# Feed-forward stages that start on tokens not yet normed, in a two-layer decoder trunk

## The chip, the cores and the metric

The kernel runs on one core of one Trainium2 chip. The metric is the device time of one execution in microseconds (us), as the median of several runs. The engines of the core are named as in the profile: PE (matrix products and transposes; PEld is its loading of weights), DVE (vector engine), ACT (scalar engine), POOL (GpSimd), SP (the engine whose queue issues the loads from memory).

## What is computed

The input is 256 tokens of 1024 values in float32. Two layers follow each other; each has a feed-forward stage, a token mixer, and a second feed-forward stage. Cut to what matters here:

```python
def rmsnorm(x, g):
    y = x * lax.rsqrt(jnp.mean(x * x, axis=-1, keepdims=True) + 1e-6)
    return y * g

def swiglu(h, w_gate, w_up, w_down):          # 1024 -> 2816 -> 1024
    return (jax.nn.silu(h @ w_gate) * (h @ w_up)) @ w_down

for layer in range(2):
    f = swiglu(rmsnorm(x, g[0]), w_gate[layer, 0], w_up[layer, 0], w_down[layer, 0])
    x = x + 0.5 * rmsnorm(f, g[1])
    x = x + rmsnorm(mixer(rmsnorm(x, g[2])), g[3])
    f = swiglu(rmsnorm(x, g[4]), w_gate[layer, 1], w_up[layer, 1], w_down[layer, 1])
    x = x + 0.5 * rmsnorm(f, g[5])
```

So there are four feed-forward stages. Below they are the first (layer 0, ahead of the mixer), the second (layer 0, behind it), the third (layer 1, which follows the second with no mixer between) and the fourth. The factor 1/rms is one number for each token, and it can be applied before the product with `w_gate` and `w_up` or to the rows of its result.

## The kernel before

**Tiles.** The tokens lie in two halves (t = 0, 1) of 128 tokens by 1024 values. For a product the tokens must stand transposed: 8 blocks of 128x128. Every product in full precision is made of three products of a coarse part (`hi`) and a remainder (`lo`): `mm3` (L144 to L147) issues them. ACT makes each `hi` as a rounded copy and DVE makes each `lo` as the difference: for weights in `split_raw` (L96, L97; 128x1024 at a time, a *unit*), for tokens in `split` (L157, L158).

**Weights.** A piece of weights (1 MB) is loaded into one of 5 raw buffers (`raw`), and its two units go to buffers `hi` and `lo`, of which there are 9 each (`NW`). A unit's buffer is free again when the last product that reads it is done.

**A feed-forward stage** (`ffn`, L250) goes over 11 chunks of 256 columns of `w_gate` and `w_up`. `GU(t, c)` (L269) is the product of one half with one chunk, 24 PE matmuls of 512 columns; `both` (L253) is the same for both halves. `gated` (L279) takes the result: Silu on ACT, a multiply on DVE (L285, or L287 where it applies 1/rms itself), giving `h`. `T` (L290) transposes `h` on PE and splits it, and `Dn` (L298) is the 12 matmuls of its product with `w_down` (rows `f<-hi_dn,hs`). Pairs of chunks (2, 3), (5, 6) and (8, 9) are done by seven products instead of eight, `M(i, a)` with i = 0 to 6 (L338), 12 matmuls each: their factors are sums of token blocks, made once for each stage by `sums` (L315: four additions L319 and four splits into `S1` to `S4`, the last in the buffer `tg`), and sums of weight blocks, made on DVE for each pair (L358, L359, L374, L382: 128x2048 each) and then split in their turn (rows `lo_t`). Results are combined on DVE too (L364, L372, L379).

The second to fourth stage begin with `GU(0,0), GU(0,1), T(0,0), Dn(0,0), GU(1,0), T(0,1), GU(1,1), T(1,0), Dn(0,1)`; then comes `M(0, 2)`, which calls `sums`. The first stage begins with `both(0), both(1)`, two `T`, and `M(0, 2)`.

**Norms.** When the last product of a stage or mixer for one half is done, `tail` (L844) calls `post_norm` (L222), which ends in the new tokens `x` (L237). Then, ahead of a feed-forward stage, `ffn_norm` (L185) runs: ACT sums the squares (L192), `rstd_of` (L179) makes 1/rms with a small DVE operation (L181) and a power on POOL (L182), ACT multiplies the tokens by it (L197), PE transposes the result (8 transposes, L153), DVE multiplies by the norm's gain `g` (L201, four 128x512 in all for both halves), and `split` gives `hi` and `lo` in `xh0/xl0` or `xh1/xl1`. The tiles from L201 are kept (`whole`) for `sums`. Ahead of a mixer, `pre_norm` (L206) transposes the tokens as they are, and the mixer applies 1/rms to its products. The first stage does both: `both(0)` runs on the tokens of `pre_norm`, in the buffers `S1`, `S2`, `S3` and `tg`, with 1/rms applied in `gated` (L287); behind it `ffn_norm` (given the ready 1/rms) makes the normed ones, and all else uses these.

**The order.** The list of `GU`, `M`, `T` and `Dn` comes from the planner in `ffn` (`price`, `settle`), and it is the same whatever happens in the norms. When the kernel is built, a scheduler gives every engine a fixed list of instructions: it plays the program through with durations of its own, and an engine that is free takes the earliest-written instruction whose inputs and output buffer are reckoned ready. So an instruction can be moved ahead of earlier-written ones that aren't ready. On the chip each engine follows its list in order.

**Elsewhere.** The conformer part of the even mixer scales its transposed channels by a number for each token with a product of the kind that the change adds: a diagonal matrix from DVE (L590), a PE product with a matrix of ones (L591), and a DVE multiply that reads the result with a broadcast (L592). The ones are a part of the constants, loaded by `small_loads` (L808) in the first stage.

Of the kernel before, what the change touches and what calls it, by code (L numbers as in the profile page):

```python
# [10 lines left out]
F32 = mybir.dt.float32  # L11
F32R = mybir.dt.float32r
BF16 = mybir.dt.bfloat16
AF = mybir.ActivationFunctionType
ALU = mybir.AluOpType
AX = mybir.AxisListType

P = 128
D = 1024
KD = D // P  # L20
# [9 lines left out]
PRE_SCALE = 1.0 / 32.0  # L30
# [9 lines left out]
C_ID, C_ONES, C_MEAN, C_CAUSW, C_ROPE, C_MNEG, C_MSTRICT = 0, 128, 256, 384, 512, 768, 1024  # L40
C_KEEP, C_END = 768, 1280
# [7 lines left out]
def trunk(ctx, tc, x, norm_g, w_gate, w_up, w_down, ab_in, ab_out, conv_w, conv_b, conv_g, conv_bb,  # L49
          cd_in, cd_out, sgu_g, sgu_b, sgu_w, sgu_bs, consts, out):  # L50
    nc = tc.nc
    cp = ctx.enter_context(tc.tile_pool(name="cp", bufs=1))
    wp = ctx.enter_context(tc.tile_pool(name="wp", bufs=1))
    sp = ctx.enter_context(tc.tile_pool(name="sp", bufs=1))
# [8 lines left out]
    def ps_tr(name):  # L63
        return pp.tile([P, 512], F32, tag="tr", name=name, bufs=2)

    xs = [cp.tile([P, D], F32, name=f"x{t}") for t in range(2)]
    cst = cp.tile([P, C_KEEP], F32, name="cst")
    ident = cst[:, C_ID:C_ID + P]
    ones = cst[:, C_ONES:C_ONES + P]
# [2 lines left out]

    mhalf = cp.tile([P, 1], F32, name="mhalf")
    nc.gpsimd.memset(mhalf, -0.5)

    early = cp.tile([P, 1], F32, name="early")
    nc.scalar.activation(early, mhalf, AF.Silu)
# [71 lines left out]
    def transposes(src, name, n=4):  # L149

        ps = ps_tr(name)
        for i in range(n):
            nc.tensor.transpose(ps[:, i * P:(i + 1) * P], src[:, i * P:(i + 1) * P], ident)  # L153
        return ps

    def split(ps, hi, lo):
        nc.scalar.activation(hi, ps, AF.Copy)  # L157
        nc.vector.tensor_tensor(lo, ps, f32v(hi), op=ALU.subtract)  # L158

    def xT_tiles(t, name):  # L160
        hi = sp.tile([P, KD, P], F32R, tag=f"xh{t}", name=f"xh{t}_{name}")
        lo = sp.tile([P, KD, P], F32R, tag=f"xl{t}", name=f"xl{t}_{name}")
        return hi, lo


    def in_turn(dst, src):

        tc.keep_in_program_order(nc.sync.dma_start(dst, src))
# [10 lines left out]
    def rstd_of(s, eps, name):  # L179
        v = sp.tile([P, 2], F32, tag="rv", name=f"v_{name}", bufs=4)  # L180
        nc.vector.tensor_scalar(v[:, 0:1], s[:, 0:1], s[:, 1:2], eps, op0=ALU.add, op1=ALU.add)  # L181
        nc.gpsimd.tensor_tensor(v[:, 1:2], v[:, 0:1], mhalf, op=ALU.pow)  # L182
        return v[:, 1:2]

    def ffn_norm(t, gi, name, r=None):  # L185

        hi, lo = xT_tiles(t, name)
        if r is None:
            s = sp.tile([P, 2], F32, tag="rs", name=f"s2_{name}{t}", bufs=4)
            for j in range(2):  # L190
                junk = sp.tile([P, 512], F32, tag="y", name=f"j2{j}_{name}{t}", bufs=2)
                nc.scalar.activation(junk, xs[t][:, j * 512:(j + 1) * 512], AF.Square, scale=PRE_SCALE, accum_out=s[:, j:j + 1])  # L192
            r = rstd_of(s, 1e-6, f"p{name}{t}")
        whole = []
        for j in range(2):
            y = sp.tile([P, 512], F32, tag="y", name=f"y{j}_{name}{t}", bufs=2)
            nc.scalar.activation(y, xs[t][:, j * 512:(j + 1) * 512], AF.Copy, scale=r)  # L197
            ps = transposes(y, f"xT{j}_{name}{t}")
            a = sp.tile([P, 512], F32, tag="tok", name=f"a{j}_{name}{t}", bufs=4)
            gk = gT[:, gi * KD + 4 * j:gi * KD + 4 * j + 4, None].to_broadcast([P, 4, P])  # L200
            nc.vector.tensor_tensor(a.rearrange("p (a b) -> p a b", b=P), ps.rearrange("p (a b) -> p a b", b=P), gk, op=ALU.mult)  # L201
            split(a, hi[:, 4 * j:4 * j + 4].rearrange("p a b -> p (a b)"), lo[:, 4 * j:4 * j + 4].rearrange("p a b -> p (a b)"))
            whole.append(a)
        return hi, lo, None, whole

    def pre_norm(t, gi, name):  # L206

        s = sp.tile([P, 2], F32, tag="rs", name=f"s2_{name}{t}", bufs=4)
        hi, lo = xT_tiles(t, name) if gi else [sp.tile([P, KD, P], F32R, tag=tag, name=f"{tag}_{name}{t}", bufs=1) for tag in (("S1", "S2"), ("S3", "tg"))[t]]
        for j in range(2):  # L210
            ps = transposes(xs[t][:, j * 512:(j + 1) * 512], f"xT{j}_{name}{t}")
            y = sp.tile([P, 512], F32, tag="y", name=f"y{j}_{name}{t}", bufs=2)
            gk = gT[:, gi * KD + 4 * j:gi * KD + 4 * j + 4, None].to_broadcast([P, 4, P])
            nc.vector.tensor_tensor(y.rearrange("p (a b) -> p a b", b=P), ps.rearrange("p (a b) -> p a b", b=P), gk, op=ALU.mult)
            split(y, hi[:, 4 * j:4 * j + 4].rearrange("p a b -> p (a b)"), lo[:, 4 * j:4 * j + 4].rearrange("p a b -> p (a b)"))
        for j in range(2):
            c = slice(j * 512, (j + 1) * 512)
            junk = sp.tile([P, 512], F32, tag="y", name=f"j2{j}_{name}{t}", bufs=2)
            nc.scalar.activation(junk, xs[t][:, c], AF.Square, scale=PRE_SCALE, accum_out=s[:, j:j + 1])
        return hi, lo, rstd_of(s, 1e-6, f"p{name}{t}"), None  # L220

    def post_norm(t, acc, g, half, name, last=False):  # L222

# [26 lines left out]
    def ffn(l, j, pre, tail, hooks=()):  # L250
        gu_u, dn_u, hT, acc = {}, {}, {}, {}

        def both(_, c):  # L253

            gu_u[c] = prep_gu(l, j, c)
            if 1 not in pre:
                pre[1] = pre_norm(1, 0, "l0f0")
            ps = [ps_mm(f"gu{l}{j}_{t}_{c}") for t in range(2)]
            for u in range(0, KD, 2):
                for t in range(2):  # L260
                    for k in (u, u + 1):
                        mm3(ps[t], pre[t][0][:, k, :], pre[t][1][:, k, :], *gu_u[c][k], k == 0, k == KD - 1)
            for t in range(2):
                gated(t, c, ps[t])
            if (l, j, c) == (0, 0, 0):
                for t in range(2):
                    pre[t] = ffn_norm(t, 0, "l0n", pre[t][2])

        def GU(t, c):  # L269
            if c not in gu_u:  # L270
                gu_u[c] = prep_gu(l, j, c)
            hi, lo = pre[t][0:2]
            ps = ps_mm(f"gu{l}{j}_{t}_{c}")
            for k in range(KD):
                wh, wl = gu_u[c][k]
                mm3(ps, hi[:, k, :], lo[:, k, :], wh, wl, k == 0, k == KD - 1)
            gated(t, c, ps)

        def gated(t, c, ps):  # L279
            r = pre[t][2]  # L280
            sg = sp.tile([P, FC], F32, tag="p", name=f"sg{l}{j}_{t}_{c}", bufs=2)
            nc.scalar.activation(sg, ps[:, 0:FC], AF.Silu, scale=1.0 if r is None else r)  # L282
            h = sp.tile([P, FC], F32, tag="pts", name=f"h{l}{j}_{t}_{c}", bufs=2)
            if r is None:
                nc.vector.tensor_tensor(h, ps[:, FC:2 * FC], sg, op=ALU.mult)  # L285
            else:
                nc.vector.scalar_tensor_tensor(h, ps[:, FC:2 * FC], r, sg, op0=ALU.mult, op1=ALU.mult)  # L287
            hT[t, c] = h
# [515 lines left out]
    def small_loads():  # L804

        for n in range(1, 6):
            in_turn(*g_rows(n))
        in_turn(cst[:, P:C_KEEP], consts[:, P:C_KEEP])  # L808
        masks = sp.tile([P, 512], F32, tag="tok", name="masks", bufs=4)
        in_turn(masks[:, 0:C_END - C_KEEP], consts[:, C_KEEP:C_END])  # L810
        nc.gpsimd.tensor_copy(mneg, masks[:, 0:2 * P])
        nc.gpsimd.tensor_copy(mstrict, masks[:, 2 * P:4 * P])
        small["cw"] = sp.tile([P, 512], F32, tag="tok", name="cw_sb", bufs=4)
        in_turn(small["cw"][0:TAPS, :], conv_w[0])
        small["cv"] = sp.tile([12, P], F32, tag="dg", name="cv_sb", bufs=2)
        for i, vv in enumerate((conv_b, conv_g, conv_bb)):
            in_turn(small["cv"][4 * i:4 * i + 4], vv[0].rearrange("(a b) -> a b", b=P))
        small["sw"] = sp.tile([P, 4, P], F32, tag="tok", name="sw_sb", bufs=4)
        in_turn(small["sw"], sgu_w[0].rearrange("g t s -> t g s"))
        small["sb"] = sp.tile([4, P], F32, tag="dg", name="sbt_sb", bufs=2)  # L820
        in_turn(small["sb"], sgu_bs[0])
# [19 lines left out]
    def tail_of(l, i_post, half, nxt, name):  # L841
        gp = {}

        def tail(t, acc):  # L844
            if not gp:
                gp["post"] = g_row(l, i_post)
            post_norm(t, acc, gp["post"], half, name, last=nxt is None)
            if nxt is not None:
                norm = pre_norm if nxt[1] == 2 else ffn_norm
                state.setdefault("next", {})[t] = norm(t, 3 * nxt[0] + nxt[1] // 2, name)  # L850
        return tail

    def step(run, *args):
# [63 lines left out]
```

## Time and profile before

| | |
|---|---|
| median of 3 runs | 991.79 us (991.43 to 992.21) |
| the profiled execution: its own time | 989.26 us |
| the profiled execution: span from first to last instruction | 987.3 us |
| mean granted PE clock | 0.994 |
| PE, DVE, ACT, POOL busy | 97%, 85%, 59%, 10% |
| moved by DMA | 175.32 MB, mean 178 GB/s |

Busy time is the time in which an engine works on at least one instruction. Matmuls overlap, so PE shown as busy can still be waiting in part. In the profile's rows a line such as L153 is that of a helper where a helper issues the instruction, so the names of the tiles (out<-in) tell the operations apart: `xT` are transposed tokens, `gu`, `gX`, `gY` results of products with gate and up weights, `f` results with down weights, `hT` transposes of `h`. Times in rows count from the start of the span.

### The profile page before, as it was taken

To read this page: it belongs to the slowest core of one execution; us is meant where nothing else is said; L and a number is where in the kernel's file an instruction comes from. 1 tells how busy PE (TensorE), PEld (TensorE's weight loads), DVE (VectorE), ACT (ScalarE), POOL (GpSimd) and SP (SyncE) were. 2 spreads that over 40 slices of the span, in tenths; PEclk is the share of its full clock that TensorE was granted. 3 is DMA by queue.
4 is the path that set the end of the run, shared out by engine and by line. 5 is a ranking of instruction groups with operands and counts; after the bars stand their busy time and mean duration, and the time that the engine had idled before them with its cause. 6 is when DMAs were issued, how large, how long until landed. Compare 5 with 4: busy or idle time off the path is not lost.

```text
span 987.3 us, 11853 instructions
## 1 busy us (share of the span) xinstructions
PE 953.1 (97%) x4350; PEld 759.0 (77%) x4352; DVE 837.7 (85%) x1022; ACT 579.4 (59%) x845; POOL 97.7 (10%) x104
## 2 busy tenths in 40 slices
PE   7999999999888999999999999999999989999997
PEld 5777888787657688878778887877787778887875
DVE  6999999679887999988789999996757489999883
ACT  7575656563535656656576756575555466656561
POOL 0100000039961000000000000000000010000000
PEclk9999999999989999999999999999999999999999
DMA  9657647456007339383862658385564142838341
GB/s 313 209 184 230 218 167 282 161 177 232 1 18 239 91 107 315 122 262 121 284 213 86 200 183 275 109 311 162 209 220 144 43 127 86 275 120 288 107 168 43
DMA packets 121754, 175.32 MB, mean 178 GB/s; under 512 B 4481, under 2 KB 96321, under 8 KB 121696
## 3 DMA queue, kind: packets, MB, share of 16 engines
q1 hardware_dynamic: 121536, 174.50, 53.7%
q8 instruction: 34, 0.56, 0.2%
q14 instruction: 24, 0.20, 0.1%
q10 hardware_dynamic: 160, 0.07, 0.0%
HBM read 173.50 MB, written 1.05 MB: 177 GB/s over the span
## 4 chain that ended last, share of the span: by engine, by line
PE 84%; DVE 8%; ACT 3%; DMA 2%; issue 2%; POOL 1%; SPq 0%; POOLq 0%; DVEq 0%; ACTq 0%
PE f L145 8%; PE f L146 8%; PE f L147 8%; PE gu L147 6%; PE gu L145 6%; PE gu L146 6%; PE gX L334 4%; PE gX L336 4%; PE gX L335 4%; PE gY L334 3%; PE gY L335 3%; PE gY L336 3%; PE hT L153 2%; PE cd L145 2%; PE cd L146 2%
## 5 line engine op out<-in xcount | busy, mean ns | idle before, releaser
L145 PE MATMUL f<-hi_dn,hs 128*128 128x512 f32 x352 | 139.7, 400 | 0.5 <-ACT hs L157 0.5
L146 PE MATMUL f<-lo_dn,hs 128*128 128x512 f32 x352 | 138.0, 392 | 0.0
L147 PE MATMUL f<-hi_dn,hs 128*128 128x512 f32 x352 | 137.5, 393 | 0.0
L96 ACT ACTIVATE hi_t<-raw_b 128x1024 fp32r<-128x1024 f32 x96 | 98.1, 1053 | 60.2 <-DVE raw_b L374 47.1
L97 DVE TENSOR_TENSOR lo_t<-raw_b,hi_t 128x1024 fp32r<-128x1024 f32 x96 | 114.5, 1220 | 14.5 <-ACT hi_t L96 14.5
L97 DVE TENSOR_TENSOR lo_dn<-raw_dn,hi_dn 128x1024 fp32r<-128x1024 f32 x88 | 105.7, 1219 | 9.0 <-ACT hi_dn L96 8.9
L96 ACT ACTIVATE hi_dn<-raw_dn 128x1024 fp32r<-128x1024 f32 x88 | 91.7, 1055 | 36.4 <-PE gu L147 26.2
L97 DVE TENSOR_TENSOR lo_gu<-raw_gu,hi_gu 128x1024 fp32r<-128x1024 f32 x80 | 96.6, 1218 | 8.3 <-ACT hi_gu L96 8.0
L96 ACT ACTIVATE hi_gu<-raw_gu 128x1024 fp32r<-128x1024 f32 x80 | 83.5, 1055 | 27.9 <-PE m L147 11.7
L97 DVE TENSOR_TENSOR lo_b<-raw_b,hi_b 128x1024 fp32r<-128x1024 f32 x72 | 86.3, 1219 | 2.5 <-ACT hi_b L96 2.3
L96 ACT ACTIVATE hi_b<-raw_b 128x1024 fp32r<-128x1024 f32 x72 | 74.8, 1057 | 21.4 <-PE gu L147 12.9
L145 PEld LDWEIGHTS f<-hi_dn,hs 128*128 128x128 f32 x352 | 65.7, 188 | 17.2 <-ACT hs L157 4.4
L147 PEld LDWEIGHTS f<-hi_dn,hs 128*128 128x128 f32 x352 | 66.1, 188 | 15.3 <-DVE hs L158 1.7
L146 PEld LDWEIGHTS f<-lo_dn,hs 128*128 128x128 f32 x352 | 66.2, 188 | 13.8 <-DVE lo_dn L97 1.0
L157 ACT ACTIVATE hs<-hT 128x256 fp32r<-128x256 f32 x88 | 32.2, 377 | 54.9 <-PE hT L153 54.9
L145 PE MATMUL gu<-hi_gu,xh_l1f 128*128 128x512 f32 x160 | 63.6, 397 | 0.0
L146 PE MATMUL gu<-lo_gu,xh_l1f 128*128 128x512 f32 x160 | 63.4, 396 | 0.0
L147 PE MATMUL gu<-hi_gu,xl_l1f 128*128 128x512 f32 x160 | 62.2, 393 | 0.0
L158 DVE TENSOR_TENSOR hs<-hT,hs 128x256 fp32r<-128x256 f32 x88 | 36.0, 418 | 20.4 <-ACT hs L157 20.0
L282 ACT ACTIVATE sg<-gu 128x256 f32<-128x256 f32 x38 | 14.5, 381 | 42.1 <-PE gu L147 39.3
L334 PE MATMUL gY<-hi_t,S 128*128 128x512 f32 x96 | 38.6, 402 | 0.0
L336 PE MATMUL gY<-hi_t,S 128*128 128x512 f32 x96 | 38.0, 396 | 0.0
(361 smaller groups left out, 2240.7 us busy)
## 6 DMA issues: line engine op xcount, KB each, us to landing
raw_dn<-in_ffn_w_down_dram SPq DMA_DIRECT2D x44, 1024.0 KB, 5.0
raw_b<-in_ffn_w_gate_dram SPq DMA_DIRECT2D x48, 512.0 KB, 4.7
raw_b<-in_ffn_w_up_dram SPq DMA_DIRECT2D x48, 512.0 KB, 6.2
raw_gu<-in_ffn_w_gate_dram SPq DMA_DIRECT2D x38, 512.0 KB, 4.2
raw_gu<-in_ffn_w_up_dram SPq DMA_DIRECT2D x38, 512.0 KB, 5.2
raw_ab<-in_ab_w_in_dram SPq DMA_DIRECT2D x10, 1024.0 KB, 6.9
raw_cd<-in_cd_w_in_dram SPq DMA_DIRECT2D x10, 1024.0 KB, 5.1
raw_abo<-in_ab_w_out_dram SPq DMA_DIRECT2D x4, 1024.0 KB, 5.5
```

The lines of the kernel that those rows point to most:

```text
L96: nc.scalar.activation(hi, r, AF.Copy)
L97: nc.vector.tensor_tensor(lo, r, f32v(hi), op=ALU.subtract)
L145: nc.tensor.matmul(ps, xh, wh, start=first, stop=False)
L146: nc.tensor.matmul(ps, xh, wl, start=False, stop=False)
L147: nc.tensor.matmul(ps, xl, wh, start=False, stop=last)
L153: nc.tensor.transpose(ps[:, i * P:(i + 1) * P], src[:, i * P:(i + 1) * P], ident)
L157: nc.scalar.activation(hi, ps, AF.Copy)
L158: nc.vector.tensor_tensor(lo, ps, f32v(hi), op=ALU.subtract)
L282: nc.scalar.activation(sg, ps[:, 0:FC], AF.Silu, scale=1.0 if r is None else r)
L334: nc.tensor.matmul(ps, A[0][:, k, :], wh[:, o], start=first and k == 0, stop=False, **tc_skip)
L335: nc.tensor.matmul(ps, A[0][:, k, :], wl[:, o], start=False, stop=False, **tc_skip)
L336: nc.tensor.matmul(ps, A[1][:, k, :], wh[:, o], start=False, stop=k == 3, **tc_skip)
```

## The change

`ffn_norm` is gone. `pre_norm` now runs ahead of feed-forward stages too (its `ffn` case): it transposes the tokens as they are, multiplies by the gain, splits into `S1`, `S2` (t = 0) or `S3`, `tg` (t = 1), keeps the products with the gain (`whole`), and only then sums the squares and makes 1/rms. The products ahead of `M(0, 2)` use these tiles, and `gated` applies 1/rms. Behind `GU(1,1)` (behind `both(1)` in the first stage, where it was behind `both(0)`) `renorm` calls the new `normed` for both halves: the diagonal matrix, the product with ones, four multiplies in place, and four splits into `xh0/xl0` and `xh1/xl1`. The ones are now written by POOL at the start, since the first stage needs them before `small_loads`.

```diff
     mhalf = cp.tile([P, 1], F32, name="mhalf")
     nc.gpsimd.memset(mhalf, -0.5)
+    nc.gpsimd.memset(ones, 1.0)
...
-    def ffn_norm(t, gi, name, r=None):
...
     def pre_norm(t, gi, name):
+        ffn = gi % 3 != 1
         s = sp.tile([P, 2], F32, tag="rs", name=f"s2_{name}{t}", bufs=4)
-        hi, lo = xT_tiles(t, name) if gi else [sp.tile([P, KD, P], F32R, tag=tag, name=f"{tag}_{name}{t}", bufs=1) for tag in (("S1", "S2"), ("S3", "tg"))[t]]
+        hi, lo = xT_tiles(t, name) if not ffn else [sp.tile([P, KD, P], F32R, tag=tag, name=f"{tag}_{name}{t}", bufs=1) for tag in (("S1", "S2"), ("S3", "tg"))[t]]
+        whole = []
         for j in range(2):
             ps = transposes(xs[t][:, j * 512:(j + 1) * 512], f"xT{j}_{name}{t}")
-            y = sp.tile([P, 512], F32, tag="y", name=f"y{j}_{name}{t}", bufs=2)
+            if ffn:
+                y = sp.tile([P, 512], F32, tag="tok", name=f"a{j}_{name}{t}", bufs=4)
+                whole.append(y)
+            else:
+                y = sp.tile([P, 512], F32, tag="y", name=f"y{j}_{name}{t}", bufs=2)
...
-        return hi, lo, rstd_of(s, 1e-6, f"p{name}{t}"), None
+        return hi, lo, rstd_of(s, 1e-6, f"p{name}{t}"), whole
+
+    def normed(t, pre, name):
+        hi, lo = xT_tiles(t, name)
+        dg = sp.tile([P, P], F32, tag="dg", name=f"dg_{name}{t}", bufs=2)
+        nc.vector.tensor_scalar(dg, ident, pre[2], None, op0=ALU.mult)
+        ps = ps_tr(f"r_{name}{t}")
+        nc.tensor.matmul(ps[:, 0:P], ones, dg, start=True, stop=True)
+        for j, a in enumerate(pre[3]):
+            v = a.rearrange("p (a b) -> p a b", b=P)
+            nc.vector.tensor_tensor(v, v, ps[:, None, 0:P].to_broadcast([P, 4, P]), op=ALU.mult)
+            split(a, hi[:, 4 * j:4 * j + 4].rearrange("p a b -> p (a b)"), lo[:, 4 * j:4 * j + 4].rearrange("p a b -> p (a b)"))
+        return hi, lo, None, pre[3]
...
         def both(_, c):
...
-            if (l, j, c) == (0, 0, 0):
-                for t in range(2):
-                    pre[t] = ffn_norm(t, 0, "l0n", pre[t][2])
+            if first and c == 1:
+                renorm()
+
+        def renorm():
+            for t in range(2):
+                pre[t] = normed(t, pre[t], f"n{l}{j}")
...
         def GU(t, c):
...
             gated(t, c, ps)
+            if (t, c) == (1, 1):
+                renorm()
...
-        in_turn(cst[:, P:C_KEEP], consts[:, P:C_KEEP])
+        in_turn(cst[:, C_MEAN:C_KEEP], consts[:, C_MEAN:C_KEEP])
...
-                norm = pre_norm if nxt[1] == 2 else ffn_norm
-                state.setdefault("next", {})[t] = norm(t, 3 * nxt[0] + nxt[1] // 2, name)
+                state.setdefault("next", {})[t] = pre_norm(t, 3 * nxt[0] + nxt[1] // 2, name)
```

## Rows read from the trace of the kernel before

**Rows 1.** The page, busy time, share of the span and instructions of each engine.

```profile
PE 953.1 (97%) x4350; PEld 759.0 (77%) x4352; DVE 837.7 (85%) x1022; ACT 579.4 (59%) x845; POOL 97.7 (10%) x104
```

**Rows 2.** PE's waits: waiting instruction <- what it waited for: us in total, times, longest.

```profile
PE xT_l1f L153 <- ACT y_l1f L197: 3.3, 3, 2.3
...
PE gu L145 <- ACT xh_l0f L157: 0.8, 1, 0.8
PE xT_l0f L153 <- ACT y_l0f L197: 0.8, 1, 0.8
...
PE gu L147 <- DVE xl_l0f L158: 0.5, 1, 0.5
```

**Rows 3.** Timeline at the start of the second stage, half t = 0.

```profile
318.46 1.42 DVE L237 SCALAR_TENSOR_TENSOR x<-tg_l0f,v_ql0f,x 128x512 f32<-128x512 f32 x2
...
321.22 0.55 POOL L182 TENSOR_TENSOR v_pl0f<-v_pl0f,mhalf 128x1 f32<-128x1 f32 x1 [2.79 <-DVE v_pl0f L181]
...
322.57 1.27 PE L153 MATMUL xT_l0f<-cst,y_l0f 128*128 128x128 f32 x8 [0.76 <-ACT y_l0f L197]
```

**Rows 4.** Stretches: PE, PEld, DVE, ACT, POOL busy (instructions), PEclk, DMA share, GB/s.

```profile
37.10:66.10 29.00, 26.81 (x122) 21.61 (x121) 27.43 (x31) 15.99 (x23) 2.48 (x2) 1.00 0.46 143
334.00:352.40 18.40, 18.40 (x85) 14.89 (x84) 16.73 (x23) 9.92 (x16) 0.00 (x0) 1.00 0.37 115
352.40:374.90 22.50, 22.50 (x102) 18.23 (x101) 20.79 (x22) 15.48 (x20) 0.00 (x0) 1.00 0.30 97
536.30:558.60 22.30, 22.30 (x101) 18.26 (x101) 20.89 (x21) 15.12 (x20) 0.00 (x0) 1.00 0.29 94
826.60:848.90 22.30, 22.30 (x101) 18.26 (x101) 21.00 (x21) 15.22 (x20) 0.00 (x0) 1.00 0.30 95
```

**Rows 5.** Timeline, stages two to four: a unit of M(4, 2)'s weights and its first matmul.

```profile
371.79 1.22 DVE L97 TENSOR_TENSOR lo_t<-raw_b,hi_t 128x1024 fp32r<-128x1024 f32 x1
...
376.44 0.40 PE L335 MATMUL gX<-lo_t,S 128*128 128x512 f32 x1
...
556.62 3.48 DVE L97 TENSOR_TENSOR lo_t<-raw_b,hi_t 128x1024 fp32r<-128x1024 f32 x3
...
560.16 0.40 PE L335 MATMUL gX<-lo_t,S 128*128 128x512 f32 x1
...
844.93 2.36 DVE L97 TENSOR_TENSOR lo_t<-raw_b,hi_t 128x1024 fp32r<-128x1024 f32 x2 [0.52 <-ACT hi_t L96]
...
850.47 0.40 PE L335 MATMUL gX<-lo_t,S 128*128 128x512 f32 x1
```

**Rows 6.** The chain that ended last, its piece of L591 (two products).

```profile
303.14 0.51 PE crstd L591 x4
```

**Rows 7.** Lines L590 and L592: duration ns min/median/max.

```profile
L590 DVE TENSOR_SCALAR dg<-cst,cv x2: 286/286/286, 302.3 to 302.8; 128x128 f32<-128x128 f32 x2
...
L592 DVE TENSOR_TENSOR cacc<-cacc,crstd x1: 1212/1212/1212, 304.2 to 304.2; 128x1024 f32<-128x1024 f32 x1
```

**Rows 8.** DVE's groups from 334 to 344 us, second stage.

```profile
L158 DVE TENSOR_TENSOR S<-a_l0f,S 128x512 fp32r<-128x512 f32 x4 | 2.8, 690 | 0.0
L319 DVE TENSOR_TENSOR a_l0f<-a_l0f,a_l0f 128x512 f32<-128x512 f32 x4 | 2.8, 689 | 0.1
...
L201 DVE TENSOR_TENSOR a_l0f<-xT_l0f,gT 128x512 f32<-128x512 f32 x2 | 1.3, 681 | 0.0
```

**Rows 9.** PE's groups from 346.6 to 352.0 us, second stage, the first.

```profile
L145 PE MATMUL gu<-hi_gu,xh_l0f 128*128 128x512 f32 x8 | 3.2, 400 | 0.0
```

**Rows 10.** Timeline, second stage: h of (1, 0) and its transposes; a weight unit's wait.

```profile
345.16 1.06 ACT L96 ACTIVATE hi_dn<-raw_dn 128x1024 fp32r<-128x1024 f32 x1 [1.57 <-PE gu L147]
...
347.40 0.42 DVE L285 TENSOR_TENSOR h<-gu,sg 128x256 f32<-128x256 f32 x1
...
352.02 0.38 PE L153 MATMUL hT<-cst,h 128*128 128x128 f32 x2
```

**Rows 11.** PE's groups from 22.5 to 37.1 us, first stage, the transposes of ffn_norm.

```profile
L153 PE MATMUL xT_l0n<-cst,y_l0n 128*128 128x128 f32 x16 | 2.3, 277 | 0.7 <-DVE a_l0n L201 0.7
```

More of the change, by code (lines that the diff above doesn't have):

```diff
@@ L183, in rstd_of, with pre_norm @@
         return v[:, 1:2]
-    def ffn_norm(t, gi, name, r=None):
[L187 to L193, printed above, removed]
+    def pre_norm(t, gi, name):
+        ffn = gi % 3 != 1
+        s = sp.tile([P, 2], F32, tag="rs", name=f"s2_{name}{t}", bufs=4)
+        hi, lo = xT_tiles(t, name) if not ffn else [sp.tile([P, KD, P], F32R, tag=tag, name=f"{tag}_{name}{t}", bufs=1) for tag in (("S1", "S2"), ("S3", "tg"))[t]]
@@ L194, in ffn_norm @@
         whole = []
         for j in range(2):
-            y = sp.tile([P, 512], F32, tag="y", name=f"y{j}_{name}{t}", bufs=2)
[L197 to L208, printed above, removed]
-        hi, lo = xT_tiles(t, name) if gi else [sp.tile([P, KD, P], F32R, tag=tag, name=f"{tag}_{name}{t}", bufs=1) for tag in (("S1", "S2"), ("S3", "tg"))[t]]
-        for j in range(2):
-            ps = transposes(xs[t][:, j * 512:(j + 1) * 512], f"xT{j}_{name}{t}")
-            y = sp.tile([P, 512], F32, tag="y", name=f"y{j}_{name}{t}", bufs=2)
+            ps = transposes(xs[t][:, j * 512:(j + 1) * 512], f"xT{j}_{name}{t}")
```

## The prediction

> **What bounds the kernel now.** I read the page first: PE is busy for 97% of the span, DVE for 85% [rows 1]. So nearly all the time is PE's, and a change pays only where PE waits, and costs where it makes PE wait. The waits of PE show what the change aims at: the transposes and first products at the start of a feed-forward stage wait 3.3 + 0.8 + 0.8 + 0.5 = 5.4 us in all [rows 2]. The timeline says why: the new tokens are ready at 319.88 us, but squares, the power on POOL and ACT's scaling stand between them and the transposes, which start at 322.57 [rows 3].
>
> The view by stretches warns of the other side. Behind GU(1,1), from 352.4 to 374.9 us, DVE is busy for 20.79 of 22.5 us, and it is much the same in the third and fourth stage [rows 4]. Here the weights of M are summed and split on DVE. How near this is to being the bound is seen by setting a unit's end on DVE beside its first matmul: the second unit for M(4,2) ends at 373.01 us and is used at 376.44, a lead of 3.4 us; in the third stage 2.3 us (the first of three units ends 1.22 us after 556.62), in the fourth 3.2 us [rows 5]. PE never stops there now, but DVE has little to give.
>
> **What is removed.** In stages two to four the chain squares, power, scaling no longer stands ahead of the transposes; 1/rms is next needed by the Silu of GU(0,0), 24 matmuls later. ACT loses the scaling (two operations of a half). I take the whole 5.4 us as gained. Bounds: 3.1 us, if the one wait of 2.3 us in it [rows 2] is a chance of this execution, and 7 us, as the products behind the waits also run closer.
>
> **What is added on PE.** A product with ones takes 0.51/2 = 0.26 us [rows 6]; six in stages two to four are 1.5 us, wholly on PE. The transposes stay, 16 for a stage.
>
> **What is added on DVE and ACT.** For each half: a diagonal matrix, 0.29 us [rows 7], two multiplies and two splits. The trace has no multiply in place with a broadcast from PSUM of this size; the nearest are L201 at 0.68 us and L592 at 1.21 us for twice the size [rows 7, 8], so 0.61 to 0.69 us, and I take 0.68. A `lo` takes 0.68 to 0.69. For both halves: 4 x 0.68 + 4 x 0.68 = 5.4 us. The diagonals need only 1/rms and can be made early, in time that DVE has. ACT gets four `hi` and loses four scalings of like size, and with 15.5 of 22.5 us busy [rows 4] it has room: nothing.
>
> **What is moved.** This term decides. `sums` reads the normed tiles, so its four additions and four splits, 4 x 0.69 + 4 x 0.69 = 5.5 us [rows 8], now come behind `normed`. Before, they ran in the ten microseconds from 334 us, hidden under GU. Where does `normed` go? Its DVE work waits for the product with ones, which is written behind GU(1,1), and PE takes later-written work only when nothing earlier is ready. The trace tells whether that happens: `h` of (1,0) is ready at 347.8 us, its two transposes are written right behind GU(1,1), and they run at 352.02, behind all 24 matmuls [rows 9, 10]. PE's list had no gap to move them into. So the product with ones will stand behind GU(1,1) too, and 5.4 + 5.5 = 10.9 us of DVE work falls between there and M(4,2), in a stretch where DVE is already full.
>
> Can DVE use the time so freed to get ahead? Hardly: at 345 us ACT's next unit waits 1.57 us for GU's matmul to free a buffer [rows 10]. All nine buffers are in use, and the units for M only find room as GU(1,0) and GU(1,1) finish. In the third stage I allow 1 us for it.
>
> So in each stage M(4,2) slips by 10.9 us, less the DVE idle of the stretch (1.7, 1.4, 1.3 us [rows 4]), less the lead (3.4, 2.3, 3.2):
> second 10.9 - 1.7 - 3.4 = 5.8; third 10.9 - 1.4 - 2.3 - 1.0 = 6.2; fourth 10.9 - 1.3 - 3.2 = 6.4; together 18.4 us. PE has nothing else to do meanwhile, since the next chunks' units come from the same DVE, and behind it PE is the bound again, so the loss stays. That `S1` to `S3` and `tg` now hold raw tokens, so that `S3` and `S4` cannot be written before GU(1,1) ends, adds nothing: they come later anyway.
>
> **The first stage** changes least: 16 transposes, 2.3 us of busy time with a wait of 0.7 [rows 11], go from in front of both(1), and `normed` goes behind it. But from 37.1 to 66.1 us DVE is busy for 27.43 of 29 us while PE has 2.2 us idle [rows 4]: DVE sets the pace, and its work stays the same but for two diagonals, 0.6 us [rows 7]. I take 0, between -3 (PE's saving kept whole) and +2 (DVE short of work before both(1) ends). The ones on POOL and the smaller load are long done when needed: nothing.
>
> **Sum.** -5.4 + 1.5 + 18.4 + 0 = +14.5 us. On the profiled execution's 989.3 us this is 1003.8. That execution lies 2.5 us under the median shown, so the forecast for the median is 1006.3 us. With the added multiplies at 0.61, leads used better and the first stage gaining, +9; with no idle absorbed and the smallest gain, +22: its own range is 1001 to 1014.
>
> **Rivals.**
> *The product with ones slips forward.* If PE's list has a gap between the power and GU(1,1) in which the scheduler sets it, `normed` and `sums` run on DVE under GU as the old work did. Only 5.4 + 0.6 = 6.0 us of DVE work is then new, against a lead of 2.3 to 3.4 and idle of 1.3 to 1.7 behind GU(1,1) and 1.67 us before it (18.4 - 16.73 [rows 4]): that is enough in the second and fourth stage and 0.6 us short in the third (1.7 + 1.4 + 2.3 = 5.4). Then -5.4 + 1.5 + 0.6 = -3.3, so 988.5 us. It decides once the multiplies are done before about 346 us. For it: there are waits of 0.5 to 0.8 us near the stage's start [rows 2], though before 1/rms is ready, and these are the ones that go. Against it: the transposes of rows 10. The Trainium skill, "Perfetto Trace Analysis", section "Optimization Strategy", says to find the gaps of the most-contended engine and let what they wait for start sooner; by that alone the change gives this rival's time. The same section says that the most-contended engine can change over time, and rows 4 bear that out.
> *Only half t = 0 slips forward.* Its 1/rms is ready earlier than that of t = 1, a whole tail. Then 2.7 us of DVE work leaves the burst in each stage: 1006.3 - 3 x 2.7 = 998 us.
> *Nothing to see.* The stall is 1 us or less in a stage because DVE gets ahead while GU runs, and eats the gain: 990 to 994 us. Against it: the buffers [rows 10].
> *Worse than forecast.* PE waits for `S2` in M(1,2) and again at M(4,2), and the late weights reach the following chunk: 3 us more in a stage, 1015 us.
>
> **How the numbers follow.** Forecast 0.66, forward slip 0.16, half slip 0.09, nothing 0.05, worse 0.04. Over 0.2% (2 us) is what a measurement of this kernel can tell from no change. Faster takes the forward slip and some of the first stage's gain with a small stall: 0.18; same 0.05; slower 0.77. The range for 8 in 10 reaches from the forward slip's time to the top of the forecast's own range: 988 to 1014, beside the likeliest one's 1001 to 1014.
>
> **What would show it.** In the new profile, PE's waits for the scaled tokens are gone, and the first GU follows the last product of the mixer closely. The product with ones stands behind GU(1,1)'s last matmul; DVE idles for some us before it and is solid from there to M(5,2). PE has waits on `lo_t` or on `S` around M(1,2) to M(4,2), 5 to 7 us in each of stages two to four, and the lead of rows 5 is near zero. Wrong: the product with ones stands among GU's matmuls, or DVE's units for M are done before GU(1,1) ends, and PE has no such wait.

## The result and the profile after

The changed kernel takes **1003.25 us** (median of 4 runs, 1002.43 to 1005.25) against 991.61 for the kernel before in the same comparison: a ratio of 1.0130, 95% interval 1.0109 to 1.0150. By that ratio it is slower by 12.9 us (10.8 to 14.9), by the two medians by 11.6, where 14.5 was forecast. Its profiled execution took 1005.25 us, 2 us above the median, with a span of 1003.4.

The page, busy time of each engine, of the changed kernel [rows 1]:

```profile
PE 962.8 (96%) x4350; PEld 762.4 (76%) x4352; DVE 853.6 (85%) x1054; ACT 574.1 (57%) x841; POOL 97.9 (10%) x105
```

DVE has 15.9 us more work, and PE 9.7 us more busy time for the same number of matmuls: part of them ran slower. PE's waits, the columns as in [rows 2]:

```profile
PE gX L339 <- ACT hi_t L97: 6.1, 4, 1.7
PE gY L339 <- ACT hi_t L97: 5.3, 3, 1.8
PE gY L339 <- ACT S L158: 3.0, 3, 1.0
```

The waits for scaled tokens are gone. In their place stand waits for weight halves and for `S`. In each of stages two to four PE waits once for `S` (1.0), once for `gX`'s weights (1.7) and once for `gY`'s (1.8): 4.5 us a stage, 13.3 in all. The fourth wait of the first row, 1.1 us, is in the first stage.

The place of the product with ones decided the forecast. PE's timeline, second stage (start, duration, instruction):

```profile
351.44 0.40 PE L148 MATMUL gu<-hi_gu,tg_l0f 128*128 128x512 f32 x1
351.67 0.61 PE L215 MATMUL r_n<-dg_n,cst 128*128 128x128 f32 x4
352.03 0.47 PE L146 MATMUL f<-hi_dn,hs 128*128 128x512 f32 x1
...
365.31 0.50 PE L339 MATMUL gY<-hi_t,S 128*128 128x512 f32 x1 [0.99 <-ACT S L158]
...
378.28 0.49 PE L339 MATMUL gX<-hi_t,S 128*128 128x512 f32 x1 [1.69 <-ACT hi_t L97]
380.55 0.80 PE L339 MATMUL gY<-hi_t,xh_n 128*128 128x512 f32 x1 [1.77 <-ACT hi_t L97]
```

It comes right behind the last matmul of GU(1,1). Both halves take 0.36 us from start to start, and the stalls follow 13.6, 26.6 and 28.9 us later. DVE's timeline in the same stretch:

```profile
352.95 2.47 DVE L218 TENSOR_TENSOR a_l0f<-a_l0f,r_n 128x512 f32<-128x512 f32 x4
355.33 2.49 DVE L159 TENSOR_TENSOR xl_n<-a_l0f,xh_n 128x512 fp32r<-128x512 f32 x4
...
358.41 0.68 DVE L324 TENSOR_TENSOR a_l0f<-a_l0f,a_l0f 128x512 f32<-128x512 f32 x1
359.01 1.22 DVE L98 TENSOR_TENSOR lo_t<-raw_b,hi_t 128x1024 fp32r<-128x1024 f32 x1
...
374.86 2.28 DVE L379 TENSOR_TENSOR raw_b<-raw_b,raw_b 128x2048 f32<-128x2048 f32 x1
377.06 2.28 DVE L387 TENSOR_TENSOR raw_b<-raw_b,raw_b 128x2048 f32<-128x2048 f32 x1
379.26 2.35 DVE L98 TENSOR_TENSOR lo_t<-raw_b,hi_t 128x1024 fp32r<-128x1024 f32 x2
```

Norming takes DVE from 352.95 to 357.7 us, when its next operation starts, and the sums only then begin. The weight difference for M(4,2) (L379) starts at 374.86, with that for M(5,2) (L387) right behind it. In the kernel before, the one for M(4,2) started 8.0 us earlier, in DVE's timeline:

```profile
366.84 2.28 DVE L374 TENSOR_TENSOR raw_b<-raw_b,raw_b 128x2048 f32<-128x2048 f32 x1
```

ACT's timeline of the changed kernel shows who waits for it:

```profile
377.17 2.00 ACT L97 ACTIVATE hi_t<-raw_b 128x1024 fp32r<-128x1024 f32 x2 [4.51 <-DVE raw_b L379]
```

ACT stands idle for 4.51 us until the difference is done. The first matmul of M(4,2) reads only a `hi` and starts at 378.28, when ACT has made the first; DVE's `lo` follow from 379.26. Before, a unit of that kind was split at 371.79, 4.7 us ahead of its matmul [rows 5]; now the matmuls are there first.

Stretches of the changed kernel's second stage and, behind the stalls, of each later one (columns as in [rows 4]):

```profile
334.00:352.40 18.40, 18.40 (x85) 14.58 (x84) 13.21 (x14) 7.06 (x10) 0.00 (x0) 1.00 0.56 172
352.40:374.90 22.50, 21.51 (x96) 16.79 (x95) 22.15 (x33) 13.87 (x21) 0.00 (x0) 1.00 0.00 0
374.90:380.00 5.10, 2.19 (x9) 1.25 (x7) 5.10 (x4) 2.57 (x3) 0.00 (x0) 1.00 0.63 209
380.00:385.00 5.00, 4.46 (x13) 3.59 (x14) 5.00 (x5) 4.28 (x5) 0.00 (x0) 0.66 0.91 283
...
570.00:575.00 5.00, 5.00 (x15) 3.98 (x16) 4.44 (x5) 4.33 (x6) 0.00 (x0) 0.66 0.99 315
...
865.00:870.00 5.00, 5.00 (x16) 3.92 (x16) 4.19 (x5) 4.09 (x6) 0.00 (x0) 0.67 1.07 351
```

Ahead of GU(1,1)'s end DVE now idles for 5.2 of 18.4 us (1.7 before); behind it DVE is full. Then comes something that the forecast did not have: behind the stalls PE is granted 0.66 or 0.67 for 5 us, a mixture of its 2.4 and 1.2 GHz levels. In the first of these stretches PE ran 13 matmuls, where the kernel before ran 26:

```profile
380.00:385.00 5.00, 5.00 (x26) 3.93 (x25) 5.00 (x8) 4.73 (x9) 0.00 (x0) 1.00 1.09 348
```

Busy time at the lower clock, 4.46 x 0.34 + 5 x 0.34 + 5 x 0.33, makes 4.9 us more over the three stages. This is read from one execution, whose mean granted clock is 0.985. The other three had 0.989, and the kernel before had 0.982 to 0.994 in its executions beside the experiments, so how much of the 4.9 us stands in the medians is not known.

### The profile page after: what moved, and what is told of

It reads as the page before. It is cut to its first block, busy times and chain, and to the rows that moved or that the text cites. A ratio compares the mean times of both kernels' runs of the same rounds, so it can differ in the third digit from the quotient of the medians.

```text
span 1003.4 us, 11865 instructions
## 1 busy us (share of the span) xinstructions
PE 962.8 (96%) x4350; PEld 762.4 (76%) x4352; DVE 853.6 (85%) x1054; ACT 574.1 (57%) x841; POOL 97.9 (10%) x105
## 4 chain that ended last, share of the span: by engine, by line
PE 84%; DVE 9%; DMA 3%; ACT 2%; issue 1%; POOL 0%; SPq 0%; POOLq 0%; DVEq 0%; ACTq 0%
PE f L146 7%; PE f L147 7%; PE f L148 7%; PE gu L146 7%; PE gu L148 7%; PE gu L147 7%; PE gX L341 4%; PE gX L339 4%; PE gX L340 4%; PE gY L339 3%; PE gY L340 3%; PE gY L341 3%; PE hT L154 2%; PE cd L148 1%; PE cd L147 1%; PE cd L146 1%
## 5 line engine op out<-in xcount | busy, mean ns | idle before, releaser
L97 ACT ACTIVATE hi_b<-raw_b 128x1024 fp32r<-128x1024 f32 x72 | 73.6, 1055 | 19.8 <-PE gu L148 15.5
L146 PE MATMUL gu<-hi_gu,xh_n 128*128 128x512 f32 x192 | 76.1, 397 | 0.0
L147 PE MATMUL gu<-lo_gu,xh_n 128*128 128x512 f32 x192 | 75.2, 392 | 0.0
L148 PE MATMUL gu<-hi_gu,xl_n 128*128 128x512 f32 x192 | 74.3, 390 | 0.0
L146 PEld LDWEIGHTS gu<-hi_gu,xh_n 128*128 128x128 f32 x192 | 36.1, 188 | 8.3 <-DVE c L397 1.3
L148 PEld LDWEIGHTS gu<-hi_gu,xl_n 128*128 128x128 f32 x192 | 36.0, 188 | 7.5
L339 PE MATMUL gY<-hi_t,S 128*128 128x512 f32 x96 | 38.7, 403 | 3.0 <-ACT S L158 3.0
```

Of the source, the lines that this page charges most:

```text
L97: nc.scalar.activation(hi, r, AF.Copy)
L146: nc.tensor.matmul(ps, xh, wh, start=first, stop=False)
L147: nc.tensor.matmul(ps, xh, wl, start=False, stop=False)
L148: nc.tensor.matmul(ps, xl, wh, start=False, stop=last)
L339: nc.tensor.matmul(ps, A[0][:, k, :], wh[:, o], start=first and k == 0, stop=False, **tc_skip)
```

## The experiments

All times are medians; a ratio is to the kernel before, run beside it (medians of 990.02 to 991.77 us), with its 95% interval. Gains and losses in us go by these ratios, times 991.6 us. The theory throughout: the start of a stage gains, and norming and sums on DVE behind GU(1,1) cost far more. The rivals put the loss elsewhere: in the products, in the first stage, in the amount of DVE work wherever it stands.

**The gain alone.** The kernel before with raw tokens at the start of stages two to four and 1/rms in the gate, but no norming afterwards: the factor 1/rms is left out from the third chunk on in these stages, so the products with ones, the multiplies and the second splits are missing and the sums can run early.

```
+            y = xs[t][:, j * 512:(j + 1) * 512]
...
+            if (t, c) == (1, 1):
+                for u in range(2):
+                    pre[u] = pre[u][0:2] + (None, pre[u][3])
```

> The kernel before, with the transposes of stages two to four taken from the tokens as they are and 1/rms applied by gated up to GU(1,1); no product with ones, no new multiplies or splits. It leaves out 1/rms in stages two to four from the third chunk on. It shows what the earlier start is worth by itself. Theory 1: 5.4 us by the waits, and up to 8.5 by the shifts in the changed kernel's trace (6.9 plus 1.5 of products with ones): 983 to 986 us. Rival (the start is gained and lost again behind GU(1,1), where DVE sets the pace): 989 to 992 us.

Measured: 983.63 us, ratio 0.9930 (0.9908 to 0.9952). The start is worth 6.9 us, and so everything that norming and its place cost is (1.0130 - 0.9930) x 991.6 = 19.8 us, with some 3 us either way by the two intervals. Behind GU(1,1) nothing stalls, with DVE little busier than in the kernel before:

```profile
334.00:352.40 18.40, 18.40 (x83) 14.78 (x82) 17.83 (x22) 8.78 (x13) 0.00 (x0) 1.00 0.53 172
352.40:374.90 22.50, 22.50 (x103) 18.46 (x102) 21.21 (x22) 15.55 (x20) 0.00 (x0) 1.00 0.30 96
```

**The late sums alone.** The kernel before, with its sums held back until `h` of GU(1,1) is there; a factor of one made from that `h` ties them to it.

```
+            if (t, c) == (1, 1):
+                one = sp.tile([P, 2], F32, tag="rv", name=f"one{l}{j}", bufs=4)
+                nc.vector.tensor_scalar(one[:, 0:1], hT[t, c][:, 0:1], 0.0, 1.0, op0=ALU.mult, op1=ALU.add)
+                held.append(one[:, 0:1])
...
+                if held and n in (1, 3):
+                    nc.vector.scalar_tensor_tensor(dst, x, held[0], y, op0=ALU.mult, op1=op)
```

> The kernel before, with only the move: in stages two to four two of the additions of sums (the others depend on them) read a one that is made from h of GU(1,1), so the 5.5 us of sums run behind GU(1,1). No added multiplies, no product with ones, no earlier start. Theory 1 with its lead: 5.6 us less idle of 1.3 to 1.7 and lead of 2.3 to 3.4 is 0.5, 1.9 and 1.1 us, so +3.5 us: 995 us (993 to 998). Theory 2 (only added work costs): 992 us. A burst that costs in full: 1008 us.

Measured: 996.92 us, ratio 1.0061 (1.0038 to 1.0085), 6.0 us slower (3.8 to 8.4). Place alone, with no arithmetic worth naming added, costs time. DVE's stretches, taken 3.6 us later because GU(1,1) ends that much later in this trace, show the shift, 5.3 us out of the first and 1.6 into the second (16.73 and 20.79 before [rows 4]); the rest runs later still:

```profile
337.60:356.00 18.40, 18.40 (x84) 14.51 (x83) 11.41 (x15) 7.89 (x12) 0.00 (x0) 1.00 0.36 115
356.00:378.50 22.50, 22.50 (x102) 18.25 (x100) 22.39 (x28) 14.78 (x21) 0.00 (x0) 1.00 0.14 48
```

With the prediction's own terms (5.5 us, less idle, less lead, less the third stage's 1.0) the same move would cost 0.4 + 0.8 + 1.0 = 2.2 us. These terms look at M(4,2) alone, and there PE did not stop. But behind the pair it waited 0.7 us for down weights in the second, third and fourth stage, 0.6 us for `h` in the third and 1.1 us for `hs` in the fourth: 3.8 us, where the kernel before waits 0.7 us. So 3.1 of the 6.0 us lie at instructions that the terms leave out; where the rest lies stays open.

**The first stage's norming moved up**, behind both(0), in the changed kernel.

```
-            if first and c == 1:
+            if first and c == 0:
                 renorm()
```

> The changed kernel with one part undone: in the first stage normed is written behind both(0) again, as ffn_norm was, and both(1) runs on normed tokens. The trace shows the first stage 2 us longer than before. If the place behind both(1) is the cause: 1001 us. If it is a chance of that execution or the other order of loads: 1003 us. In both the waits in stages two to four stay at 5 us and more each.

Measured: 1005.78 us, ratio 1.0153 (1.0118 to 1.0188). No gain: that place is not where the time goes. Nor do the 2 us of the expectation tell of the change: the first new tokens behind the first stage are written at 190.2 us in the changed kernel's trace and at 188.1 in that of the kernel before, but at 190.8 and 190.5 in the traces of the two kernels above, which have the old first stage.

**Norming moved up in stages two to four.** In the changed kernel, `normed` is written behind GU(0,1) instead of GU(1,1), and its tiles are swapped in when GU(1,1) is done. The arithmetic is the same.

```
+            if (t, c) == (0, 1):
+                done.extend(normed(u, pre[u], f"n{l}{j}") for u in range(2))
             if (t, c) == (1, 1):
-                renorm()
+                pre.update(enumerate(done))
```

> The changed kernel with one move: in stages two to four the diagonal, the product with ones, the multiplies and the splits are written behind GU(0,1), and the normed tiles are only used from GU(1,1) on, as before; S1 to S3 and tg still hold the raw tokens. Theory 1 (the place: 10.9 us of DVE work falls behind GU(1,1)): the gains at the stage starts stay (some 7 us in the profile), the waits of PE in M(1,2) to M(5,2) go, and only the first stage's loss of 2 us stays: 987 us (984 to 991). Theory 2 (the work itself: 5.4 us of DVE in each stage, wherever it stands): still slower than before, 997 to 1003 us. Theory 3 (the buffers: S3 and tg are held by raw tokens until GU(1,1) ends, so sums is late anyway): 1 to 3 us of waits on S stay in each stage, 990 to 996 us.

Measured: 993.75 us, ratio 1.0046 (1.0029 to 1.0064). By the ratios 8.3 us came back by moving alone, but 987 was missed. The time is that of the third theory, 990 to 996, but of its waits on `S` none is left. PE's waits say what is left, two of 1.7 us each in the second and in the third stage and one of 1.2 in the fourth; the sixth, 1.0, is in the first stage. (The 3.8 us a stage of the next expectation are too many.)

```profile
PE gY L342 <- ACT hi_t L97: 4.6, 3, 1.7
PE gX L342 <- ACT hi_t L97: 4.4, 3, 1.7
```

and DVE's timeline says why:

```profile
334.79 0.69 DVE L218 TENSOR_TENSOR a_l0f<-a_l0f,r_n 128x512 f32<-128x512 f32 x1 [2.15 <-PE r_n L215]
...
352.39 2.29 DVE L366 TENSOR_TENSOR raw_b<-raw_b,raw_b 128x2048 f32<-128x2048 f32 x1
```

DVE stands 2.15 us in its order waiting for the product with ones, and behind all the norming a weight difference for M(1,2) (L366, 2.29 us) starts only at 352.39, behind GU(1,1).

**Both halves at their own place.** As the last, with half t = 0 normed behind GU(0,0) and t = 1 behind GU(0,1).

```
-            if (t, c) == (0, 1):
-                done.extend(normed(u, pre[u], f"n{l}{j}") for u in range(2))
+            if t == 0 and c < 2:
+                done.append(normed(c, pre[c], f"n{l}{j}"))
```

> The changed kernel with the first token tile normed behind GU(0,0) and the second behind GU(0,1); nothing else differs from the run that had both behind GU(0,1) (993.75 us), which still stalled 3.8 us a stage for the weight blocks' first halves, with VectorE waiting 2.15 us in its order for the product with ones and the weight sum of the second pair member (L366 there) slid behind GU(1,1). Theory 1, the loss is VectorE's work that stands behind GU(1,1), whatever slid there: with both products ready before VectorE comes to them that sum goes back ahead of GU(1,1), and 2 to 4 us a stage come back: 984 to 988 us. Rival, what is left is the amount of VectorE work between the stage's start and the pair, wherever it stands: 992 to 995 us, as before the split.

Measured: 986.86 us, ratio 0.9961 (0.9941 to 0.9980), and once more beside the next run:

> The kernel with the split places once more, beside the one with the old first stage: 985.5 to 988 us, under the kernel before by 0.2 to 0.6%.

986.64 us, ratio 0.9963 (0.9946 to 0.9979). This version beats both kernels: by some 4 us the one before, by some 16.6 the changed one, though its DVE does as much as the changed kernel's (852.5 and 853.6 us busy). Its product with ones for the second half, L366 and stretches (those of the second stage taken 3.7 us earlier, as GU(1,1) ends earlier here):

```profile
333.93 0.38 PE L215 MATMUL r_n<-dg_n,cst 128*128 128x128 f32 x2
```

```profile
337.77 2.28 DVE L366 TENSOR_TENSOR raw_b<-raw_b,raw_b 128x2048 f32<-128x2048 f32 x1
```

```profile
330.30:348.70 18.40, 18.40 (x86) 15.03 (x85) 17.98 (x24) 9.96 (x15) 0.00 (x0) 1.00 0.52 172
348.70:371.20 22.50, 22.50 (x102) 18.24 (x100) 21.71 (x23) 13.27 (x19) 0.00 (x0) 1.00 0.14 48
533.00:555.30 22.30, 22.30 (x100) 18.02 (x99) 21.55 (x24) 13.00 (x18) 0.00 (x0) 1.00 0.14 48
821.50:843.80 22.30, 22.30 (x101) 18.24 (x100) 21.90 (x24) 14.09 (x20) 0.00 (x0) 1.00 0.14 48
```

The weight difference is done 14.6 us earlier than in the run above, DVE is busy ahead of GU(1,1)'s end, and PE is busy for all of the stretch behind it in all three stages; in the second and third a wait of 1.2 us for a `hi` of M(5,2) comes right behind. The rival that only the amount of DVE work counts, 992 to 995 us, is out. Nor can the loss come from the raw tokens in `S1` to `S3` and `tg`, for GU(1,1) reads them there in this version too.

**The first stage of the kernel before** in this faster version (its `ffn_norm` back, called behind both(0)).

```
-            if first and c == 1:
-                renorm()
+            if first and c == 0:
+                for t in range(2):
+                    pre[t] = ffn_norm(t, 0, "l0n", pre[t][2])
```

> The kernel with the split places (986.86 us), and its first stage as in the kernel before: normed tokens transposed anew behind both(0). Theory 1, the first stage gives and costs nothing here, as the prediction had it (between -3 and +2 us): 985 to 988 us. Rival, the first stage loses behind its second chunk what it gains ahead of the pair and more (its marks in the profile: 3.6 us early at the first pair's first product, 2.3 us late at its last), and the old one is better: 983 to 985 us.

Measured: 986.37 us, ratio 0.9959 (0.9942 to 0.9976), level with 986.64. The first stage gives and costs nothing that can be seen here.

**Sums on GpSimd.** The four additions of `sums` go to GpSimd, in the changed kernel and in the faster version.

```
-                nc.vector.tensor_tensor(dst, x, y, op=op)
+                nc.gpsimd.tensor_tensor(dst, x, y, op=op)
```

> The changed kernel with the four additions of the token sums on GpSimd instead of VectorE. Theory 1, the burst's price is VectorE's time: 2.8 us of 10.9 less a stage, so up to 8.4 us less: 995 to 998 us. Rival, the sums' lateness: they start at about 358 us in the second stage, S2 is the third of them and comes out at about 366.5 with its split, where the product that reads it stood at 364: PE waits 2 to 3 us longer for S and some 2 to 3 us shorter for the weight blocks: 1001 to 1006 us.

> As the kernel with the split places, and the four additions of the token sums (0.69 us each on VectorE) go to GpSimd; its 128x256 addition takes 1.15 us in the trace of the kernel before, so some 2.3 us each here, 9 us in a row (an estimate). Theory 1: 2.8 us of VectorE work a stage less behind GU(1,1), and if stalls are left there they shrink by that much: 983 to 987 us, at most 3 us under the split places alone. Rival, the sums in a row on the slower engine come too late for the second member of the pair, which reads S2 first: PE waits for S, 2 to 5 us a stage, 993 to 1003 us.

Measured: in the changed kernel 1014.42 us, ratio 1.0244 (1.0208 to 1.0279), worse than either theory had it; in the faster version 1000.42 us, ratio 1.0105 (1.0072 to 1.0137), as its rival had it in size, though the wait was another. Timelines of the second, one fence for each engine, GpSimd's first:

```profile
342.24 9.06 POOL L327 TENSOR_TENSOR a_l0f<-a_l0f,a_l0f 128x512 f32<-128x512 f32 x4 [10.16 <-issue]
```

```profile
345.49 0.63 ACT L158 ACTIVATE S<-a_l0f 128x512 fp32r<-128x512 f32 x1 [3.23 <-POOL a_l0f L327]
346.03 1.04 ACT L97 ACTIVATE hi_dn<-raw_dn 128x1024 fp32r<-128x1024 f32 x1
349.97 0.63 ACT L158 ACTIVATE S<-a_l0f 128x512 fp32r<-128x512 f32 x1 [2.90 <-POOL a_l0f L327]
350.51 1.04 ACT L97 ACTIVATE hi_dn<-raw_dn 128x1024 fp32r<-128x1024 f32 x1
351.46 0.46 ACT L290 ACTIVATE sg<-gu,v_pl0f 128x256 f32<-128x256 f32 x1
```

```profile
344.23 2.31 DVE L98 TENSOR_TENSOR lo_dn<-raw_dn,hi_dn 128x1024 fp32r<-128x1024 f32 x1
347.11 1.68 DVE L98 TENSOR_TENSOR lo_dn<-raw_dn,hi_dn 128x1024 fp32r<-128x1024 f32 x1 [0.56 <-ACT hi_dn L97]
351.95 0.48 DVE L295 SCALAR_TENSOR_TENSOR h<-gu,v_pl0f,sg 128x256 f32<-128x256 f32 x1 [3.16 <-ACT sg L290]
```

```profile
360.14 0.44 PE L154 MATMUL hT<-cst,h 128*128 128x128 f32 x2 [3.66 <-DVE h L295]
```

The split of `S` stands in ACT's order, so ACT waits 3.23 and 2.90 us for GpSimd's row of 9.06 us, and the Silu behind it starts at 351.46. DVE waits 3.16 us for that Silu, and its later `h` then comes too late for PE. DVE gave away 2.8 us of additions and lost more than that to waiting. That the four additions took the 9 us of the estimate is chance: its 1.15 us is a mean over two sizes, and the 128x512 additions of the kernel before took 1.36 us on average. In the changed kernel PE waits 2.5 us for `S`, 2.3 for a weight half and 1.4 for a copy by ACT in the second stage, 6.2 where it waited 4.5; the rest of that loss was not taken apart.

## Why the prediction was right

**The start's gain: right in sign, too small.** The page's waits for scaled tokens are gone. Forecast 5.4 us, with 3.1 to 7 as bounds; the run with the gain alone measured 6.9 (4.8 to 9.1 by its interval), near the upper bound.

**The products with ones: right in sign, 0.4 us too large.** Forecast 1.5 us for six; two take 0.36, six some 1.1.

**The operations on DVE: each right, their sum too large.** A multiply by the broadcast in PSUM was put at 0.68 us between 0.61 and 0.69. But four of them and four `lo` leave DVE free at 357.7 us after 4.8 us, because the end of one overlaps the start of the next; the forecast of 5.4 added them singly. The eight of the sums do the same, with 0.60 us from one start to the next (358.41 and 359.01): 4.8 us for 5.5. So the term of 10.9 us measured 9.6.

**The place: right, and it carried the result.** The product with ones stands behind GU(1,1), as the two transposes of [rows 10] had foretold, and the experiments that move `normed` and nothing else give back 8.3 and 16.6 us. So the forward slip that was the main rival did not happen by itself, and written into the kernel it is real: 986.7 us where the rival gave 988.5.

**The size of the stall: 18.4 forecast, 19.8 less 1.1 for the products = 18.7 measured, and that it came so close is luck.** Two errors cancel. The term of 10.9 us was 9.6: with that, the same working gives 9.6 - 1.7 - 3.4 = 4.5 us in the second stage, 4.9 in the third and 5.1 in the fourth, 14.5 in all, where PE's waits are 4.5 in each (5.8 to 6.4 forecast), 13.3 in all. And for the lower clock behind the waits, 4.9 us more in the profiled execution, the working had no term. Its terms "less the DVE idle, less the lead" thus come near the waits here, though PE waits in M(1,2) and M(5,2) too and not in M(4,2) alone. They are no rule: for the late sums alone they give 2.2 us against 6.0, as they leave out what comes late behind M(4,2).

**The first stage: 0 forecast**, and in the faster version the kernels with the old and the new one are level.

By the runs the change is -6.9 + 1.1 + 18.7 = 12.9 us, where the forecast had -5.4 + 1.5 + 18.4 = 14.5; most of the difference is the gain's term, taken 1.5 us too small. How DVE's idle, the leads and ACT's buffers share the stall between them stays open: no run takes these apart. Buffers of their own for the raw tokens, and more than nine weight buffers, were not tried.

## What to carry to other kernels

A wait of the busiest engine can be removed and the time still rise, if the work that made it wait is only put off: look where the put-off instructions land, and at the next engine's busy share in that very stretch. Work that needs one late value can be written as early as that value exists, each half at its own place, while a later result is still being computed; here that turned 1.3% slower into 0.4% faster with the same instructions. Before handing work to an idle engine, look at which queues must then wait for its results in order.

## What the runs showed of the hardware

**Short stalls of PE cost more than their length.** Waits of 1.7 and 1.8 us close together, with PE busy for 2.19 of 5.1 us, were followed by 5 us at a mean granted clock of 0.66, and in the third and fourth stage it was the same. The cost in the changed kernel, some 1.6 us a stage, is more than a third of the waits themselves. In the kernel with norming moved up behind GU(0,1), two waits of 1.7 us in the second and third stage were followed by a clock of 0.66 and 0.74; a single wait of 1.2 us in the fourth, at 853 us, was not:

```profile
375.00:380.00 5.00, 4.18 (x11) 3.31 (x12) 5.00 (x5) 4.56 (x5) 0.00 (x0) 0.66 0.85 270
565.00:570.00 5.00, 5.00 (x17) 3.95 (x17) 4.20 (x5) 4.09 (x6) 0.00 (x0) 0.74 1.08 352
855.00:860.00 5.00, 5.00 (x23) 4.13 (x22) 5.00 (x6) 5.00 (x8) 0.00 (x0) 1.00 1.09 357
```

**DVE slows while GpSimd adds.** A subtraction of 128x1024 took 1.22 us in the kernel before [rows 5], and 2.31 and 1.68 us beside GpSimd's row of additions. In the changed kernel with sums on GpSimd the same shows within four splits of `S`. GpSimd's timeline, and then DVE's durations for `S` (ns, least, median, most):

```profile
357.70 6.88 POOL L324 TENSOR_TENSOR a_l0f<-a_l0f,a_l0f 128x512 f32<-128x512 f32 x4 [25.85 <-PE gX L341]
```

```profile
L159 DVE TENSOR_TENSOR S<-a_l0f,S x4: 691/1532/1774, 360.0 to 365.3; 128x512 fp32r<-128x512 f32 x4
```

Three of them start while GpSimd still adds and take over 1.5 us; the last starts at 365.3, when it is done, and takes 0.69. The Trainium skill, "SBUF — State Buffer", section "SBUF: two separate sides", says that GpSimd and a DVE operation with two SBUF inputs share a pair of ports that one holds for a whole instruction while the other waits. The longer times agree with it; no row shows the port itself.
